# Half heads of attention between feed-forward groups, and a first token half that leads by 12 groups instead of 8

## The chip, the cores and the metric

The kernel runs on one NeuronCore of a Trainium2 chip. Its engines work from their own instruction queues, each in order: TensorE (PE; its weight loads are PEld) multiplies, VectorE (DVE), ScalarE (ACT) and GpSimd (POOL) do the rest, and SyncE (SP) issues every DMA of this kernel. The metric is the device time of one execution in microseconds (us). [...]

## The reference

Two layers over 1024 tokens of width 1024, in float32. Each layer:

```python
h = rms_norm(x) * (1 + sc1) + sh1
z = h @ w_in                        # split into the inputs of A, B and C
o_a = softmax attention             # 6 heads, 2 key heads, axial rotary, normed q and k
o_b = rms_norm(softmax(q1 k1) v - lam * softmax(q2 k2) v)   # 6 heads
o_c = gated linear recurrence, both directions              # 4 heads
x = x + g1 * (concat(o_a, o_b, o_c) @ w_out)
h = rms_norm(x) * (1 + sc2) + sh2
x = x + g2 * (square(relu(h @ w_ff1)) @ w_ff2)              # 1024 -> 4096 -> 1024
```

The six vectors sh1, sc1, g1, sh2, sc2, g2 of a layer are a modulation: `silu(c) @ w_mod + b_mod`. A last rms_norm ends the program.

## The kernel before

Activations lie with features on the 128 partitions and tokens along the free side, in two halves of 512 tokens. Weight products run as three float32r matmuls (`mm3`, L301 to L303): a high and a low part of the weights (`w_hi`, `w_lo`) against a high and a low part of the activations. A weight unit of 128x1024 (`wunit`) is one DMA of 512 KB on SP into `w_raw`, a cast on ACT (L295) and a subtraction on POOL (L297).

In a layer the token list `ORDER` names the jobs in program order: projections, early B heads, the recurrence `C`, then attention. `A01` is the pair 0 of A heads for the second token half, `B21` pair 2 of B heads for the second half, and so on. A block of 128 queries is a score product (L464), a maximum on DVE (L470), an exponential on ACT (L472), transposes on PE (L488) copied out by ACT or DVE (L489), and the product with V (L496). A B head has two score products a block and combines the two probability tiles on DVE (L604) or POOL. Scores use two buffers in PSUM.

Behind attention stand the output projection of the first half (`out_proj(0, ...)`), its norm (`norm_mod`), and the feed-forward part in 16 groups of two 128-wide blocks. A group of one half is a first product `ff1` (48 matmuls), squared relu, and a second product `ff2` (48 matmuls, added to x on DVE at L1150, or L1154 where it uses the wide PSUM tiles). With `LH = 8` the first half does groups 0 to 6 alone; then comes the second half's projection, group 7, then groups 8 to 15 for both halves with one load of their weights (`ffn_both`), and last groups 0 to 7 for the second half, their weights loaded a second time. `hook` issues the next layer's modulation, two of twelve pieces after each of six shared groups: a piece is eight DMAs of 256 KB (`mw`) and eight DVE multiply-adds (L234).

Program order is not the order that runs. A scheduler goes through a modelled timeline and gives each engine the earliest instruction in the program that is ready, so later work fills gaps of earlier work, with some parts raised (`hp`). All attention stood ahead of the first half's projection and feed-forward in the program, and they fill its gaps. The scheduler's result is fixed when the kernel is built; every engine then runs its list in order, and waits where the model was wrong.

Of the kernel before, what the change touches and what calls it, by code (L numbers as in the profile page):

```python
# [36 lines left out]
XAT, SAT = 4, 7  # L37
NIN = 4
MB = 9
LH = 8  # L40
OPRE = (3, 4, 5)
DEFER = (False, False)
MODAUX = 0
# [11 lines left out]
FORD = "xawn"  # L55
HP = {"C": 1000, "in": 1000, "post": 1000, "start": 3000, "start1": 1200}
ORDER = """b0 m lm v0 m B00 v1 bk1 m bq1 m bk2 B10 bq2 B20 lb m ff m fb m ci ak aq0 aq1
aq2 m cq0 cg0 cq1 cg1 C A00 A10 A20 A01 A11 A21 B01 B21 B11"""
RAWA = 1
BPOOL = ((1, 1, 1), (1, 1, 1))  # L60
MWB = 2
# [97 lines left out]
def tile_hybrid_encoder(ctx: ExitStack, tc: tile.TileContext, I, out, depth=DEPTH, dbg=None):  # L159
# [358 lines left out]
    def attention_a(ap, l, heads, hq):  # L518
        s = scr[l]
        hs = slice(hq * HALF, (hq + 1) * HALF)  # L520
        for h in heads:
            g = h // 3
            if ap.get("ag") != (g, hq):
                ap["ag"] = (g, hq)
                ks = ap["kst"].tile([P, S], F32R, name="ks", tag="kst")
                for i in range(2):
                    dma(ks.bitcast(F32)[64 * i:64 * i + 64, :], s.ak[i, g * 64:(g + 1) * 64, :])
                ap["ak"], ap["av"] = ks, load_v(ap, s, g)
            ks, vt = ap["ak"], ap["av"]
            if h % 2 == 0:  # L530
                ap["o"] = ap["O"].tile([P, HALF], F32, name="o", tag="o")
                ap["rr"] = ap["sm"].tile([P, 8], F32, name="rr", tag="rr", bufs=2)
            o, rr = ap["o"], ap["rr"]
            src = s.aq[h // 2]
            qs = []
            for i in range(2):
                q = ap["qst"].tile([P, HALF], F32R, name="qs", tag="qst")
                for r in range(2):
                    dma(q.bitcast(F32)[64 * r:64 * r + 64, :], src[i, (h % 2) * 64:(h % 2) * 64 + 64, hs])
                qs.append(q)  # L540
            pts = []
            for qp in range(2):
                pts.append(pt_tiles(ap))
                for qb in range(2):
                    b = 2 * qp + qb
                    c = (h % 2) * 4 + b
                    col = ap["sm"].tile([P, 4], F32, name="col", tag="col")
                    with hp('sm'):
                        p = sm_exp(ap, sm_scores(qs, ks, slice(b * P, (b + 1) * P)), col[:, 0:1], rr[:, c:c + 1])
                    with hp('ts'):  # L550
                        transpose_out(p, pts[qp], qb, (nc.scalar.copy, nc.vector.tensor_copy))
            with hp('pv'):
                pv(vt, pts, o, h % 2)
            if h % 2 == 1:
                nc.vector.reciprocal(rr, rr)
                rp = auxt()
                rt = token_rows(ap, rr, AF.Copy, 1.0, rp)
                for b in range(4):
                    nc.tensor.matmul(rp[:, b * P:(b + 1) * P], sel[:, b, :], rt, start=True, stop=True)
                nc.vector.tensor_mul(o, o, rp)  # L560
                for q in range(2):
                    o_store(ap["tp"], o, slice(q * 256, q * 256 + 256), l, h // 2, hq)

    def attention_b(ap, l, lamc, subg, heads, hq):
        s = scr[l]
        hs = slice(hq * HALF, (hq + 1) * HALF)
        for h in heads:
# [17 lines left out]
            for qp in range(2):  # L585
                pts.append(pt_tiles(ap))
                for qb in range(2):
                    b = 2 * qp + qb
                    sl = slice(b * P, (b + 1) * P)
                    c = (h % 2) * 4 + b  # L590
                    col = ap["sm"].tile([P, 4], F32, name="col", tag="col")
                    nm1, nm2, z2, r2 = [col[:, i:i + 1] for i in range(4)]
                    z1 = rr[:, c:c + 1]
                    with hp('sm'):
                        p1 = sm_exp(ap, sm_scores([st[0][0]], st[0][1], sl), nm1, z1)
                    with hp('sm'):
                        p2 = sm_exp(ap, sm_scores([st[1][0]], st[1][1], sl), nm2, z2)
                    nc.vector.reciprocal(r2, z2)
                    nc.vector.scalar_tensor_tensor(r2, z1, lamc, r2, op0=ALU.mult, op1=ALU.mult)
                    if b < BPOOL[hq][h // 2]:  # L600
                        nc.scalar.activation(p2, p2, AF.Copy, scale=r2)
                        nc.gpsimd.tensor_add(p1, p1, p2)
                    else:
                        nc.vector.scalar_tensor_tensor(p1, p2, r2, p1, op0=ALU.mult, op1=ALU.add)  # L604
                    with hp('ts'):
                        transpose_out(p1, pts[qp], qb, (nc.scalar.copy, nc.scalar.copy))
            with hp('pv'):
                pv(vt, pts, o, h % 2)
            if h % 2 == 1:
# [3 lines left out]
                for q in range(2):  # L613
# [8 lines left out]
                    rstd_tile(mp[:, 0:256], 1.0 / 64, sq, y, t, nc.gpsimd, 0.0)  # L622
                    nc.vector.scalar_tensor_tensor(o[:, cs], o[:, cs], subg, y, op0=ALU.mult, op1=ALU.mult)
                    o_store(tp, o, cs, l, 3 + h // 2, hq)


    def silu_store(tp, ps, half, dst, scale):
# [287 lines left out]
    for l in range(depth):  # L915
# [136 lines left out]

        def attend(tok):
            k, pr, hq = tok[0], int(tok[1]), int(tok[2])
            with hp("att"):
                if k == "A":
                    attention_a(ap, l, (2 * pr, 2 * pr + 1), hq)
                else:
                    ap["ag"] = None
                    attention_b(ap, l, lamc, subg, (2 * pr, 2 * pr + 1), hq)  # L1060

        def load_o(half, pool, rows, oT=None):
            if oT is None:
# [6 lines left out]
        for tok in ORDER.split():  # L1070
# [16 lines left out]
                    scan_c(c_["c"], b_["c"], l, pc[:, 3:4], lambda: early.append(early_weights()))  # L1087
                bctx.close()
            elif tok[0] in "AB":
                attend(tok)  # L1090
            else:
                jobs[tok]()

# [60 lines left out]
                        nc.vector.scalar_tensor_tensor(x, sp[:, k * HALF:k * HALF + n], g2[:, j - 1 + k:j + k], x,  # L1154
                                                       op0=ALU.mult, op1=ALU.add)

        def ffn_half(xh, h, groups, wide, finish=None):
            groups = list(groups)
            if not groups:
                return  # L1160
            prev = ff1(h, w1_units(groups[0]))
            for k, g in enumerate(groups):
                nxt = ff1(h, w1_units(groups[k + 1])) if k + 1 < len(groups) else None
                w2 = w2_units(g)
                if finish is None or nxt is not None:
                    ff2(xh, w2, prev, wide)
                else:
                    for c0 in range(0, HALF, TAILW):
                        ff2(xh, w2, prev, wide, c0, TAILW)
                        finish(slice(c0, c0 + TAILW))  # L1170
                prev = nxt

        def ffn_both(xa, ha, xb, hb, groups, hook):
# [18 lines left out]
            tiles = norm_tiles(npool)  # L1192
            if not last:
                nxt.append(norm_out(h_["h"]))
            ffn_half(xb, hb, range(LH), True, lambda cs: tail(1, xb, cs, tiles))

        nxt = []

        def tail(half, xh, cs=slice(0, HALF), tiles=None):
# [14 lines left out]
            for j in range(KT):  # L1214
# [5 lines left out]
                    nc.vector.scalar_tensor_tensor(x, x, fing[:, j:j + 1], y, op0=ALU.mult, op1=ALU.mult)  # L1220
                dma(out[j * P:(j + 1) * P, ts], x)

        def hook(g):
            modulation_sums()
            if l + 1 < depth and 0 <= g - LH < 6:
                modulation(l + 1, mpool, (2 * (g - LH), 2 * (g - LH) + 1), False)

        x0, h0 = out_proj(0, f_["x"], o_["h"], heads0, [j for j in range(KT) if j not in OPRE])
        ffn_half(x0, h0, range(LH - 1), False)
        actx.close()  # L1230
        hctx, h_ = open_pools([("h", f"h{l + 1}", 2 if last else 4, B)])
        xctx, x_ = open_pools([("x", f"xb{l}", KT, B)] + ([] if last else [("m", f"m{l}", 1, B)]))
# [65 lines left out]
```

## Time and profile before

| | |
|---|---|
| median of 3 runs | 3336.83 us (3336.62 to 3339.34) |
| the profiled execution | 3341.17 us, its span 3339.4 us |
| PE busy | 3154.9 us, 94% |
| DVE, ACT, POOL busy | 59%, 44%, 41% |
| mean granted clock of PE | 0.966 |

A row of the windows view gives, for a stretch of the span, its length, then the busy time and the instructions of PE, PEld, DVE, ACT and POOL, the granted clock of PE, and the share and rate of the DMA engines. A row of a timeline gives the start, the duration, engine, line, operation, what is written and read, and in brackets how long the engine stood idle before it and what it waited for. A row of the lines view gives count, busy time and mean duration in ns. Layer 0 runs to some 1710 us; its first-half projection begins at 804 us, its second-half one at 1099 us. Layer 1's begin at 2423 and 2723 us.

### The profile page before, as it was taken

What the parts mean: (1) busy time and instruction counts of PE and PEld (TensorE: products, weight loads), DVE (VectorE), ACT (ScalarE), POOL (GpSimd) and SP (SyncE); (2) the same over time, 40 slices, a digit from 0 to 9 for tenths busy, and PEclk for the clock granted to TensorE, in tenths of its full rate; (3) what the DMA queues carried; (4) which work ended last, traced back from release to release, by engine and by line L of the source; (5) the groups of instructions that cost most, each with busy time, mean ns of one, the idle gap of its engine ahead of it and who ended that gap; (6) DMA issues with size and microseconds to landing.
All of it is one profiled execution on the core that took longest, in us unless ns stands there. A gap on an engine that the chain in (4) does not pass through costs nothing. (4 is left out here: it accounts for less than half of the span.)

```text
span 3339.4 us, 44728 instructions
## 1 busy us (share of the span) xinstructions
PE 3154.9 (94%) x16561; PEld 2549.6 (76%) x16561; DVE 1979.6 (59%) x2648; ACT 1477.1 (44%) x2844; POOL 1355.8 (41%) x875
## 2 busy tenths in 40 slices
PE   5989889999899999999999998899999999999998
PEld 3978667777677888887878876777777788888786
DVE  7477866557764565546463776655567545333545
ACT  4245665656663322114233666565567423121323
POOL 3454511234345433225545642223344453333454
PEclk7989989999999999999999999899998999999999
DMA  6566356334424234413234533834343421111222
GB/s 240 166 184 209 102 163 189 105 114 143 133 86 170 89 117 136 139 57 108 94 108 135 179 121 107 245 103 133 108 130 103 146 103 63 51 51 51 80 94 80
DMA packets 215608, 411.78 MB, mean 123 GB/s; under 512 B 36056, under 2 KB 92504, under 8 KB 215392
## 3 DMA queue, kind: packets, MB, share of 16 engines
q1 hardware_dynamic: 215392, 408.93, 38.6%
q8 instruction: 131, 2.15, 0.3%
q14 instruction: 85, 0.70, 0.1%
HBM read 335.43 MB, written 73.40 MB: 122 GB/s over the span
## 5 line engine op out<-in xcount | busy, mean ns | idle before, releaser
L297 POOL TENSOR_TENSOR w_lo<-w_raw,w_hi 128x1024 fp32r<-128x1024 f32 x272 | 665.6, 2455 | 695.3 <-ACT w_hi L295 662.3
L301 PE MATMUL mm<-h_hi,w_hi 128*128 128x512 f32 x1472 | 596.9, 407 | 16.3 <-ACT h_hi L363 9.2
L302 PE MATMUL mm<-h_lo,w_hi 128*128 128x512 f32 x1472 | 587.0, 399 | 10.7 <-POOL h_lo L366 4.1
L303 PE MATMUL mm<-h_hi,w_lo 128*128 128x512 f32 x1472 | 582.9, 397 | 1.3 <-POOL w_lo L297 1.3
L295 ACT CAST w_hi<-w_raw 128x1024 fp32r<-128x1024 f32 x272 | 281.2, 1048 | 623.2 <-PE S L302 245.2
L470 DVE TENSOR_REDUCE col<-S 128x1 f32<-128x1024 f32 x288 | 348.1, 1220 | 158.7 <-PE S L464 157.7
L1154 DVE SCALAR_TENSOR_TENSOR x<-S,modc,x 128x512 f32<-128x512 f32 (+1 forms) x416 | 283.4, 725 | 229.5 <-PE S L303 229.3
L472 ACT ACTIVATE pr<-S,col 128x1024 f32<-128x1024 f32 x288 | 323.3, 1123 | 131.5 <-DVE col L470 64.8
L1131 DVE TENSOR_TENSOR ff_r<-ff_r 128x512 f32<-128x512 f32 x128 | 184.4, 1442 | 306.5 <-ACT act L1130 306.0
L301 PEld LDWEIGHTS mm<-h_hi,w_hi 128*128 128x128 f32 x1472 | 282.6, 192 | 87.7 <-ACT h_hi L363 11.2
L302 PEld LDWEIGHTS mm<-h_lo,w_hi 128*128 128x128 f32 x1472 | 281.9, 192 | 83.5 <-POOL h_lo L366 6.3
L303 PEld LDWEIGHTS mm<-h_hi,w_lo 128*128 128x128 f32 x1472 | 281.5, 191 | 64.9 <-POOL w_lo L297 2.0
L1132 POOL TENSOR_TENSOR act<-ff_r,act 128x512 fp32r<-128x512 f32 x128 | 168.7, 1318 | 399.0 <-DVE ff_r L1131 397.2
L301 PE MATMUL S<-act,w_hi 128*128 128x512 f32 (+1 forms) x832 | 318.8, 384 | 3.1 <-DVE x L1154 2.9
L302 PE MATMUL S<-act,w_hi 128*128 128x512 f32 (+1 forms) x832 | 317.6, 382 | 1.5 <-POOL act L1132 1.5
L303 PE MATMUL S<-act,w_lo 128*128 128x512 f32 (+1 forms) x832 | 314.9, 382 | 0.8 <-POOL w_lo L297 0.8
L464 PE MATMUL S<-ks,qs 128*128 128x512 f32 x768 | 247.6, 431 | 33.2 <-ACT pr L472 17.6
L488 PE MATMUL aux<-cst,pr 128*128 128x128 f32 x1536 | 235.0, 288 | 24.8 <-DVE pr L604 8.8
L1129 ACT ACTIVATE ff_r<-mm 128x512 f32<-128x512 f32 x128 | 76.1, 595 | 400.4 <-PE mm L303 392.7
L488 PEld LDWEIGHTS aux<-cst,pr 128*128 128x128 f32 x1536 | 189.2, 148 | 71.2 <-issue 17.5
L416 PE MATMUL mm<-w_hi,h_hi 128*128 128x256 f32 x640 | 186.3, 292 | 16.1 <-ACT z L639 10.6
L496 PE MATMUL aux<-pt,vt 128*64 128x256 f32 x1536 | 198.6, 385 | 1.5 <-ACT pt L489 1.5
(234 smaller groups left out, 5832.2 us busy)
## 6 DMA issues: line engine op xcount, KB each, us to landing
w_raw<-in_w_ff SPq DMA_DIRECT2D x192, 512.0 KB, 3.3
mw<-in_w_mod SPq DMA_DIRECT2D x160, 256.0 KB, 3.0
ks<-bk SPq DMA_DIRECT2D x192, 128.0 KB, 3.1
lf<-g_st SPq DMA_DIRECT2D x64, 256.0 KB, 2.8
oT<-o SPq DMA_DIRECT2D x64, 256.0 KB, 5.1
lf<-lf SPq DMA_DIRECT2D x16, 1024.0 KB, 5.3
w_raw<-in_w_out SPq DMA_DIRECT2D x32, 512.0 KB, 3.4
w_raw<-in_w_feat SPq DMA_DIRECT2D x28, 512.0 KB, 4.0
```

The costliest lines, as they stand in the source:

```text
L295: nc.scalar.copy(hi, raw)
L297: nc.gpsimd.tensor_sub(lo, raw, hi.bitcast(F32))
L301: nc.tensor.matmul(ps, wh, ah, start=first, stop=False)
L302: nc.tensor.matmul(ps, wh, al, start=False, stop=False)
L303: nc.tensor.matmul(ps, wl, ah, start=False, stop=last)
L416: nc.tensor.matmul(o, hi[:, kt, ts], uh[:, ws], start=kt == 0, stop=False)
L464: nc.tensor.matmul(sp[:, hh * HALF:(hh + 1) * HALF], q[:, sl], ks[:, hh * HALF:(hh + 1) * HALF], start=i == 0, stop=i == len(qs) - 1)
L470: nc.vector.tensor_reduce(nm, sp, axis=AX.X, op=ALU.max, negate=True)
L472: nc.scalar.activation(p, sp, AF.Exp, bias=nm, accum_out=z)
L488: nc.tensor.transpose(tp[:, j * P:(j + 1) * P], p[:, kt * P:(kt + 1) * P], ident)
L496: nc.tensor.matmul(ps[64 * c:64 * c + 64, 0:256], vt[:, kt, :], pts[c][kt // 4][:, kt % 4, :], start=kt == 0, stop=kt == KT - 1)
L1154: nc.vector.scalar_tensor_tensor(x, sp[:, k * HALF:k * HALF + n], g2[:, j - 1 + k:j + k], x, op0=ALU.mult, op1=ALU.add)
```

## The change

`LH` goes from 8 to 12: the first half does groups 0 to 10 alone, four groups are shared, and the second half does twelve at the end. Of the second half's attention only `A01` stays in `ORDER`; `LATE` holds the other five pairs. `attention_a` and `attention_b` become generators that stop after each half head (two query blocks), so a pair is four units and `LATE` twenty. Four units follow the first-half projection, and `between` gives out the other sixteen evenly over 23 places: after each `ff1` and after each `ff2` of the first half's groups. The modulation's pieces are dealt singly: two after each of the first two shared groups, one after each of the others, and the rest in the last twelve groups (`behind`, every second place).

```diff
-LH = 8
+LH = 12
 ORDER = """b0 m lm v0 m B00 v1 bk1 m bq1 m bk2 B10 bq2 B20 lb m ff m fb m ci ak aq0 aq1
-aq2 m cq0 cg0 cq1 cg1 C A00 A10 A20 A01 A11 A21 B01 B21 B11"""
+aq2 m cq0 cg0 cq1 cg1 C A00 A10 A20 A01"""
+LATE = "B01 A11 B21 A21 B11"
+AFTER_OUT = 4
...
+                if qp == 0:
+                    yield
             with hp('pv'):
                 pv(vt, pts, o, h % 2)
...
+            yield
...
-        def ffn_half(xh, h, groups, wide, finish=None):
+        def ffn_half(xh, h, groups, wide, finish=None, between=lambda: None):
...
             prev = ff1(h, w1_units(groups[0]))
+            between()
             for k, g in enumerate(groups):
                 nxt = ff1(h, w1_units(groups[k + 1])) if k + 1 < len(groups) else None
+                between()
                 w2 = w2_units(g)
...
+                between()
                 prev = nxt
...
-            ffn_half(xb, hb, range(LH), True, lambda cs: tail(1, xb, cs, tiles))
+            ffn_half(xb, hb, range(LH), True, lambda cs: tail(1, xb, cs, tiles), behind)
...
+        mleft = [] if last else list(range(12))
+        turn = [0]
+        def mod_next():
+            modulation_sums()
+            if mleft:
+                modulation(l + 1, mpool, (mleft.pop(0),), False)
         def hook(g):
-            modulation_sums()
-            if l + 1 < depth and 0 <= g - LH < 6:
-                modulation(l + 1, mpool, (2 * (g - LH), 2 * (g - LH) + 1), False)
+            for _ in range(2 if g - LH < 2 else 1):
+                mod_next()
+        def behind():
+            turn[0] += 1
+            if turn[0] % 2 == 0:
+                mod_next()
+        late = (u for tok in LATE.split() for u in attend(tok))
+        nlate = 4 * len(LATE.split()) - AFTER_OUT
+        slots = 2 * (LH - 1) + 1
+        done = [0, 0]
+        def between():
+            done[0] += 1
+            while done[1] * slots < done[0] * nlate and done[1] < nlate:
+                next(late)
+                done[1] += 1
         x0, h0 = out_proj(0, f_["x"], o_["h"], heads0, [j for j in range(KT) if j not in OPRE])
-        ffn_half(x0, h0, range(LH - 1), False)
+        for _ in range(AFTER_OUT):
+            next(late)
+        ffn_half(x0, h0, range(LH - 1), False, None, between)
+        for _ in late:
+            pass
```

The lines of the changed kernel stand a little lower: L488 is L490 there, L464 L466, L301 L303, L470 L472, L604 L609, L338 L340, L1111 L1119, L293 L295.

First place: PE in layer 0, from the last matmul of the first-half projection (it reads `oT`) to the first of the feed-forward part (it reads `h_hi`). `S` are scores, `cst,pr` transposes, `pt,vt` the product with V, `n_acc` the norm's sum. Before:

```order
L303 MATMUL mm<-oT,w_lo 128x512
L488 MATMUL aux<-cst,pr 128x128 x4
L464 MATMUL S<-ks,qs 128x512 x2
L488 MATMUL aux<-cst,pr 128x128 x4
L464 MATMUL S<-ks,qs 128x512 x2
L488 MATMUL aux<-cst,pr 128x128 x8
L464 MATMUL S<-ks,qs 128x512 x2
L340 MATMUL mm<-n_acc,cst 128x512
L496 MATMUL aux<-pt,vt 64x256 x16
L464 MATMUL S<-ks,qs 128x512 x4
L488 MATMUL aux<-cst,pr 128x128 x8
L464 MATMUL S<-ks,qs 128x512 x4
```

The same place of the changed kernel:

```order
L305 MATMUL mm<-oT,w_lo 128x512
L498 MATMUL aux<-pt,vt 64x256 x16
L490 MATMUL aux<-cst,pr 128x128 x4
L466 MATMUL S<-ks,qs 128x512 x4
L342 MATMUL mm<-n_acc,cst 128x512
L490 MATMUL aux<-cst,pr 128x128 x4
L466 MATMUL S<-ks,qs 128x512 x4
L490 MATMUL aux<-cst,pr 128x128 x8
L466 MATMUL S<-ks,qs 128x512 x6
L303 MATMUL mm<-h_hi,w_hi 128x512 x2
```

The filler is about as much as before, and differently placed: the product with V has moved ahead of the norm's sum.

Second place: DVE in layer 0, from the last residual add of that projection (`x`) to the norm's first step behind its sum. Before:

```order
L1111 SCALAR_TENSOR_TENSOR x<-mm,modc_73,x 128x512
L598 RECIPROCAL col<-col 128x1
L470 TENSOR_REDUCE col<-S 128x1
L599 SCALAR_TENSOR_TENSOR col<-rr,lam_0_518,col 128x1
L604 SCALAR_TENSOR_TENSOR pr<-pr,col 128x1024
L338 TENSOR_TENSOR n_acc<-n_acc,n_sq 128x512
L470 TENSOR_REDUCE col<-S 128x1 x2
L598 RECIPROCAL col<-col 128x1
L599 SCALAR_TENSOR_TENSOR col<-rr,lam_0_518,col 128x1
L311 TENSOR_SCALAR n_acc<-mm 128x512
```

In the changed kernel:

```order
L1119 SCALAR_TENSOR_TENSOR x<-mm,modc_73,x 128x512
L340 TENSOR_TENSOR n_acc<-n_acc,n_sq 128x512
L501 COPY o<-aux 64x256
L472 TENSOR_REDUCE col<-S 128x1 x2
L313 TENSOR_SCALAR n_acc<-mm 128x512
```

The attention work between the residual add and the last sum of squares is gone from there; two reduces still stand ahead of the norm's next step.

Third place: SP in layer 0, where the next layer's modulation is loaded (`mw`) beside the feed-forward weights (`w_raw`). Before, in the shared groups:

```order
L223 DMA mw<-in_w_mod 128x512 x16
L293 DMA w_raw<-in_w_ff 128x1024 x4
L223 DMA mw<-in_w_mod 128x512 x16
L293 DMA w_raw<-in_w_ff 128x1024 x4
L223 DMA mw<-in_w_mod 128x512 x16
```

In the changed kernel, in the second half's groups at the end of the layer:

```order
L225 DMA mw<-in_w_mod 128x512 x6
L295 DMA w_raw<-in_w_ff 128x1024 x2
L225 DMA mw<-in_w_mod 128x512
L295 DMA w_raw<-in_w_ff 128x1024
L225 DMA mw<-in_w_mod 128x512 x2
L295 DMA w_raw<-in_w_ff 128x1024
L225 DMA mw<-in_w_mod 128x512 x5
L295 DMA w_raw<-in_w_ff 128x1024 x2
L225 DMA mw<-in_w_mod 128x512
```

There are now four weight units to eight modulation loads, where there were four to sixteen, and the two kinds alternate.

## Rows read from the trace of the kernel before

**Rows 1.** The page's totals: busy us, share of the span, instructions of each engine.
```profile
PE 3154.9 (94%) x16561; PEld 2549.6 (76%) x16561; DVE 1979.6 (59%) x2648; ACT 1477.1 (44%) x2844; POOL 1355.8 (41%) x875
```
**Rows 2.** Windows by stage: stretch and length, then PE, PEld, DVE, ACT, POOL, PEclk, DMA.
```profile
700.00:804.40 104.40, 99.65 (x677) 77.15 (x676) 66.25 (x109) 64.04 (x167) 41.34 (x45) 0.98 0.44 130
804.40:881.20 76.80, 70.80 (x366) 54.05 (x365) 54.17 (x63) 45.42 (x79) 37.85 (x21) 1.00 0.49 148
881.20:904.90 23.70, 14.67 (x70) 8.66 (x69) 18.54 (x25) 17.32 (x29) 6.00 (x3) 0.79 0.31 92
904.90:945.00 40.10, 38.71 (x190) 29.95 (x191) 29.66 (x36) 28.66 (x49) 18.53 (x10) 0.95 0.25 79
945.00:1012.00 67.00, 67.00 (x359) 52.59 (x358) 42.66 (x58) 39.24 (x69) 30.86 (x19) 1.00 0.28 88
1012.00:1099.00 87.00, 86.47 (x377) 70.19 (x376) 37.91 (x48) 23.58 (x31) 45.46 (x25) 1.00 0.48 168
2417.00:2495.00 78.00, 76.14 (x411) 59.37 (x407) 46.86 (x59) 48.87 (x84) 37.62 (x20) 0.98 0.42 130
2495.00:2518.00 23.00, 14.88 (x57) 9.37 (x57) 20.64 (x30) 18.15 (x36) 5.84 (x6) 0.74 0.36 103
2518.00:2717.00 199.00, 196.67 (x953) 154.24 (x953) 124.07 (x146) 98.17 (x162) 99.79 (x54) 0.99 0.37 120
2800.00:3100.00 300.00, 300.00 (x1314) 246.25 (x1313) 113.32 (x137) 61.74 (x84) 103.50 (x57) 1.00 0.15 50
```
**Rows 3.** Timeline of PE in layer 0's norm stretch, at the lower clock.
```profile
885.73 1.19 PE L464 MATMUL S<-ks,qs 128*128 128x512 f32 x2 [3.94 <-DMA qs<-bq]
887.62 1.94 PE L488 MATMUL aux<-cst,pr 128*128 128x128 f32 x8 [0.69 <-DVE pr L604]
```
**Rows 4.** Timeline of PE in a feed-forward group with attention, at full clock.
```profile
962.72 1.03 PE L488 MATMUL aux<-cst,pr 128*128 128x128 f32 x8
963.51 0.48 PE L303 MATMUL mm<-h_hi,w_lo 128*128 128x512 f32 x1
963.83 0.40 PE L301 MATMUL mm<-h_hi,w_hi 128*128 128x512 f32 x1
```
**Rows 5.** Waits of PE, the longest in total: us, times, longest.
```profile
PE S L464 <- ACT pr L472: 17.6, 17, 2.0
```
**Rows 6.** Timeline of DVE in the norm stretch of layer 0, then of layer 1.
```profile
881.47 0.73 DVE L1111 SCALAR_TENSOR_TENSOR x<-mm,modc,x 128x512 f32<-128x512 f32 x1
...
887.39 0.68 DVE L338 TENSOR_TENSOR n_acc<-n_acc,n_sq 128x512 f32<-128x512 f32 x1
...
2495.76 0.74 DVE L1111 SCALAR_TENSOR_TENSOR x<-mm,modc,x 128x512 f32<-128x512 f32 x1
...
2499.02 1.08 DVE L338 TENSOR_TENSOR n_acc<-n_acc,n_sq 128x512 f32<-128x512 f32 x1
```
**Rows 7.** Timeline of POOL and DVE in layer 1's output projection.
```profile
2471.20 2.39 POOL L297 TENSOR_TENSOR w_lo<-w_raw,w_hi 128x1024 fp32r<-128x1024 f32 x1 [7.98 <-ACT w_hi L295]
2471.24 3.43 DVE L604 SCALAR_TENSOR_TENSOR pr<-pr,col 128x1024 f32<-128x1024 f32 x1
```
**Rows 8.** Timeline of PE and SP behind layer 0's last attention matmul.
```profile
1011.14 0.49 PE L621 MATMUL aux<-oq,cst 128*128 128x128 f32 x2
...
1029.08 3.48 SPq L1067 DMA_DIRECT2D oT<-o  x5
```
**Rows 9.** Lines by form, 945 to 1012 us: count, busy us, mean ns, idle before.
```profile
L470 DVE TENSOR_REDUCE col<-S 128x1 f32<-128x1024 f32 x10 | 12.1, 1218 | 2.4 <-PE S L464 2.4
L1150 DVE SCALAR_TENSOR_TENSOR x<-mm,modc,x 128x512 f32<-128x512 f32 x16 | 11.8, 744 | 5.1 <-PE mm L303 5.0
L604 DVE SCALAR_TENSOR_TENSOR pr<-pr,col 128x1024 f32<-128x1024 f32 x5 | 6.6, 1314 | 0.2
```
**Rows 10.** Timeline of SP, layer 0's shared groups.
```profile
1242.57 27.90 SPq L223 DMA_DIRECT2D mw<-in_w_mod  x16
...
1321.44 11.47 SPq L293 DMA_DIRECT2D w_raw<-in_w_ff  x4
```

More of the change, by code (lines that the diff above doesn't have):

```diff
@@ L606, in attention_b @@
                         transpose_out(p1, pts[qp], qb, (nc.scalar.copy, nc.scalar.copy))
+                if qp == 0:
+                    yield
             with hp('pv'):
@@ L624, in attention_b @@
                     o_store(tp, o, cs, l, 3 + h // 2, hq)
+            yield
     def silu_store(tp, ps, half, dst, scale):
@@ L1054, in attend @@
             k, pr, hq = tok[0], int(tok[1]), int(tok[2])
[L1055 to L1060, printed above, removed]
+            if k == "A":
+                yield from attention_a(ap, l, (2 * pr, 2 * pr + 1), hq)
+            else:
+                ap["ag"] = None
+                yield from attention_b(ap, l, lamc, subg, (2 * pr, 2 * pr + 1), hq)
         def load_o(half, pool, rows, oT=None):
@@ L1089, in tile_hybrid_encoder @@
             elif tok[0] in "AB":
-                attend(tok)
+                for _ in attend(tok):
+                    pass
             else:
@@ L1221, in tail @@
                 dma(out[j * P:(j + 1) * P, ts], x)
-        def hook(g):
-            modulation_sums()
-            if l + 1 < depth and 0 <= g - LH < 6:
-                modulation(l + 1, mpool, (2 * (g - LH), 2 * (g - LH) + 1), False)
-        x0, h0 = out_proj(0, f_["x"], o_["h"], heads0, [j for j in range(KT) if j not in OPRE])
-        ffn_half(x0, h0, range(LH - 1), False)
+        mleft = [] if last else list(range(12))
[4 more added lines that the diff above has]
+                modulation(l + 1, mpool, (mleft.pop(0),), False)
+        def hook(g):
+            for _ in range(2 if g - LH < 2 else 1):
[13 more added lines that the diff above has]
+                done[1] += 1
+        x0, h0 = out_proj(0, f_["x"], o_["h"], heads0, [j for j in range(KT) if j not in OPRE])
+        for _ in range(AFTER_OUT):
+            next(late)
+        ffn_half(x0, h0, range(LH - 1), False, None, between)
+        for _ in late:
+            pass
         actx.close()
```

## The prediction

> **What bounds the kernel now.** I read the engine totals first: TensorE is busy 3154.9 of 3339.4 us [rows 1], so at most 184 us of idle time and whatever it loses at the low clock can be had. The question is how much of that lies where the change works. The table of busy time by stage answers it [rows 2]. Its first six rows are layer 0: end of the recurrent scan, first-half output projection, the norm behind it, the first feed-forward work, the rest of the groups that still carry attention, and the pure groups up to the second output projection. Then layer 1: output projection, norm, all groups of the first half; the last row is feed-forward alone in the tail. A stage's length less its PE column is idle time.
>
> The reader is to see that attention inside feed-forward groups costs almost nothing already: 67.0 of 67.0 us busy in layer 0's third group stretch, 199.0 less 196.7 = 2.3 us idle in layer 1. The losses stand before that. Layer 0: output projection 76.8 - 70.8 = 6.0 us, norm 23.7 - 14.7 = 9.0, first groups 1.4. Layer 1: 1.9 and 23.0 - 14.9 = 8.1. The granted clock falls at the same place: 0.79 and 0.74 in the two norm stretches, 0.95 behind the first. [...] Before it fell the engine had stood still: 3.94 us ahead of a score matmul, after which eight transposes took 1.94 us [rows 3], against 1.03 us for eight at full clock [rows 4].
>
> [...]
>
> **The change part by part.**
> *Output projection.* In layer 0 PE's rows between its first and last matmul held 56 transposes, 28 score matmuls and 32 of P times V; now 28, 10 and none; in layer 1 64, 32, 32 become 12, 2, 7. Attention is what made PE wait there: the largest wait in the list, scores behind the exponential that frees their buffer, is 17 waits of about 1.0 us [rows 5]. Layer 1's 1.9 us with a full load is the nearest row for a good outcome, so layer 0 goes from 6.0 to about 1.9: -4.1 us (bounds 0 and -6.0). Layer 1: nothing.
> *Norm.* The chain from the last residual add to the first normed tile can't be moved; the filler can. In layer 0 DVE added the last column tile at 881.47 and reached the last sum of squares at 887.39, 5.9 us later, with attention's reduce and combine between; in layer 1 the same took 2495.76 to 2499.02, 3.3 us [rows 6]. In the changed order of DVE nothing stands between those two in layer 0, but the square on ACT is still needed. One add and one square are some 1.4 us, so 5.9 becomes about 2. The PE filler behind the last projection matmul (16 P times V, 16 transposes, 14 scores before the first feed-forward matmul) is about what it was. I take -4 us for layer 0 (bounds +2 and -9.0) and 0 for layer 1, whose order has as many DVE rows in the chain as before (bounds +3 and -8.1).
> [...]
> *Groups with attention.* The last score matmul stood 210 (layer 1: 234) feed-forward matmuls into the first half's 672; now it stands 582 (774) into 1056. At 300/1314 = 0.228 us a matmul [rows 2] that is 85 and 123 us more of mixed work. The idle rate of layer 1's groups, 2.3 in 199 us, makes that +2.4; I write +3 (bounds 0 and the rival below).
> *Switches.* After transposes a matmul starts 0.32 us before the next instead of 0.23 [rows 4], 0.09 each. Counted over PE's whole order there are 1087 changes of kind before and 1108 after: +1.9 us.
> *Scan.* A pair of B heads now stands in the scan where an A pair stood. B has twice the reduces for the same transposes. That stage idles 4.8 of 104.4 us and DVE is at 63% there [rows 2]; I take +1 a layer, +2 (bounds 0 and +6).
> *Weights.* Four more groups a layer are loaded twice: 32 more units of 512 KB, 32 x 2.39 us [rows 7] = 76 us of POOL. In the tail, POOL is busy 103.5 of 300 us and PE idles 0 [rows 2]; cost 0, and if the cover failed it would be the queue rival below.
> *Wait added.* Second-half projection now follows layer 1's last attention by 156 matmuls, 35 us (before 348, 79 us). In layer 0 the last attention matmul began at 1011.14, and the last of the sixteen loads of its output left the queue by 1032.56 [rows 8]: 21 us. The cover holds; with one such chain more behind it, some 10 us would be lost once.
>
> Sum: -4.1 - 4 - 6 + 3 + 1.9 + 2 = -7.2 us. The profiled run took 3341.17 us (span 3339.4), 4.3 over the median of 3336.83. 3341.17 - 7.2 = 3334.0, less 4.3 is 3329.7; I say 3329.
>
> [...] DVE's combine of two probability tiles takes 1.31 us on average [rows 9], but one that began 0.04 us after a weight subtraction on POOL took 3.43 [rows 7]: 2.39 of POOL's time and its own 1.0. [...]
>
> **Rivals.**
> 1. *The loss only stays put.* [...] For it: both layers lose 8 to 9 us in the norm though their fillers differ. Then -4 and -6 go: -7.2 + 10 = +2.8, 3340 against the median; without the scan and group terms 3335. I put this case at 3335 to 3340, no change.
> 2. *DVE becomes the bound in the second feed-forward product: slower.* Before, attention had precedence over all feed-forward work and filled both products; now the first product of a group is ahead of the half head behind it, and in layer 1's order 48 matmuls in a row carry no attention, so a group's attention falls into the other 48 (10.9 us). There DVE has 8 residual adds x 0.744 = 6.0 and, for some 0.7 of a B head, 5.6 reduces x 1.218 + 2.6 combines x 1.314 = 10.2 [rows 9], 16.2 us before POOL's holds; PE has 10.9 + 8.5 (a head's attention matmuls are about 12 us). It decides when DVE with its holds passes 19.4 us, which takes 1.4 holds of 2.4. If each of some 16 such products then waits 1.5 us (one or two waits of the size of [rows 5]) it costs 24 us in place of the 3: -7.2 + 21 = +13.8, 3351. Against it: 67 us without idle at DVE 64% in layer 0 [rows 2], and an order that sets 6 to 12 feed-forward matmuls between most score pairs.
> 3. *The load queue starves layer 0's last groups.* Six modulation pieces now run beside the doubled weight loads. On SP sixteen of their loads took 27.9 us and four weight loads 11.5 [rows 10]: 14.0 + 11.5 = 25.5 us a group against 96 x 0.228 = 21.9. Six groups fall behind by 21 us. Four units in store, one group's work, cover most, and the changed order mixes the two kinds, so their waits overlap. I price it at +8: the gain is gone, 3337.
> [...]
> That the change isn't done as described holds in part: the scheduler pulls the first two late pieces (B01 and A11) ahead of the projection, so three are spread, over about six to eight of the eleven groups.
>
> **Numbers.** Forecast (3321 to 3332) 0.42, rival 1 0.20, rival 2 0.17, rival 3 0.08, rival 4 0.13. What can be told from no change is 0.2%, 6.7 us: faster means below 3330.2, slower above 3343.5. Rival 4 and most of the forecast (0.38) make 0.51 faster; rivals 1 and 3 and the rest of the forecast 0.32 same; rival 2 0.17 slower. The likeliest case alone is 3321 to 3332. The range has to hold most of rivals 1, 3 and 4 and the near part of 2: 3312 to 3348.
>
> **What would show it.** Right: in the changed profile layer 0's output projection idles about 2 us, its norm stretch about 5, and the clock there is nearer 0.9; the groups with attention idle under 2 us a layer. Wrong: a norm stretch of 9 us idle at 0.79 (rival 1); DVE near 90% with score waits behind the exponential all along the groups (rival 2); weight waits of TensorE in the last groups of layer 0 (rival 3); or idle time ahead of layer 1's second output projection (the cover).

## The result, and the profile after

The changed kernel took 3358.22 us (median of six runs, 3352.48 to 3374.21); the kernel before, on the same chip in turn with it, 3338.45 (3336.62 to 3350.75). The ratio is 1.0069, 95% interval 1.0048 to 1.0090: slower by some 20 us. The forecast was 3329, with 3312 to 3348 as its range.

The run that was profiled with the comparison is the slowest of the six (3374.21), so the same kernel was profiled once more: 3359.24 us, near the median. "After" below is this second profile, 18.1 us above the profiled run of before (3341.17). Its line numbers lie 2 to 8 above those of before. Its totals, against [rows 1]:
```profile
PE 3161.0 (94%) x16561; PEld 2549.5 (76%) x16561; DVE 2021.8 (60%) x2648; ACT 1509.1 (45%) x2876; POOL 1447.3 (43%) x907
```
The same 16561 matmuls and 2648 VectorE instructions; GpSimd has 32 more, the doubled weight units. Its windows by stage (columns as in [rows 2]): layer 0's scan, output projection, norm, two stretches of groups; then layer 1's scan, projection, norm and groups.
```profile
535.91:807.75 271.84, 263.85 (x1746) 204.90 (x1745) 170.88 (x276) 176.47 (x506) 95.64 (x110) 0.99 0.42 123
807.75:866.40 58.65, 51.60 (x232) 41.67 (x230) 31.73 (x36) 27.70 (x46) 32.55 (x18) 0.94 0.55 166
866.40:890.10 23.70, 20.13 (x95) 14.62 (x95) 22.54 (x31) 18.56 (x32) 4.97 (x4) 0.78 0.42 122
890.10:930.20 40.10, 40.10 (x200) 30.95 (x199) 22.75 (x25) 19.56 (x35) 18.29 (x13) 1.00 0.24 79
930.20:1030.00 99.80, 99.80 (x503) 78.35 (x502) 56.76 (x67) 44.53 (x71) 45.78 (x25) 1.00 0.32 101
...
2163.24:2434.99 271.75, 262.55 (x1725) 204.26 (x1724) 167.26 (x276) 176.61 (x505) 93.55 (x109) 0.98 0.44 130
2434.99:2482.60 47.61, 47.61 (x223) 38.73 (x222) 15.15 (x17) 17.39 (x26) 27.89 (x15) 1.00 0.38 126
2482.60:2505.60 23.00, 16.06 (x91) 10.29 (x90) 21.09 (x27) 17.00 (x30) 8.12 (x5) 0.90 0.32 106
2505.60:2704.60 199.00, 199.00 (x987) 155.52 (x987) 123.36 (x140) 97.05 (x159) 89.32 (x49) 0.99 0.31 98
```
And the two scans of the kernel before, from the first main matmul of the scan to the first one of the output projection:
```profile
536.37:804.45 268.08, 263.29 (x1765) 205.38 (x1765) 161.23 (x261) 167.03 (x487) 90.66 (x108) 0.99 0.40 121
2151.25:2423.00 271.75, 268.71 (x1807) 209.33 (x1805) 158.25 (x263) 169.33 (x488) 87.44 (x106) 0.99 0.39 121
```
Read the layer 1 scan first: 271.75 us in both kernels, but 1725 TensorE instructions where there were 1807. The stage is as long and does 82 instructions less, and VectorE is busy 9 us longer in it. What the scan no longer does, the groups behind it must. Length alone hides this, so the table takes from each stage's length what its matmuls cost at full clock (count of a kind by its spacing in the timelines where the granted clock is 1.00: 0.2265 us for 512 columns, 0.0985 a transpose, 0.1125 P times V, 0.1 the scan's small ones), and then the same of before. A price is a typical spacing, so a cell is an estimate good to 1 or 2 us and a sum to 3 or 4. The runs behind the columns come from several chips, while the profile of before is one run (3341.17); "elsewhere" is for the most part the start of the program.

| us lost, against before | after | late_a_first | b01_early | b01_single | lead12_only | lead12_again |
|---|---|---|---|---|---|---|
| scan, layer 0 / 1 | +7.4 / +9.9 | +1.5 / -1.7 | +9.5 / +14.9 | 0 / +5.2 | +0.7 / -4.6 | +3.0 / -5.3 |
| projection, norm, groups, layer 0 | +1.3 | +3.0 | -2.5 | -3.6 | +4.0 | +4.1 |
| the same, layer 1 | -5.4 | -2.8 | -8.9 | -8.0 | -0.8 | -0.6 |
| layer 0's tail | +3.5 | +2.6 | -0.6 | -0.6 | +2.5 | +3.6 |
| layer 1's input projection | +0.5 | +0.2 | -0.8 | +0.6 | +3.1 | +8.1 |
| elsewhere | -0.4 | -6.8 | -4.9 | -0.4 | -5.7 | -4.9 |
| time of that run | 3359.24 | 3340.40 | 3351.55 | 3327.05 | 3340.62 | 3350.51 |

In the first column the two scans lose 17.3 us, and the whole column is 16.8: what the other stages lose and gain cancels, with 5.4 gained in layer 1 behind its scan. Layer 0's tail has one wait that before has only in small. The timeline of TensorE after, then of before, at the first group that only the second half runs:
```profile
1469.35 0.39 PE L303 MATMUL S<-act,w_hi 128*128 128x512 f32 x1
1476.06 0.80 PE L304 MATMUL S<-act,w_hi 128*128 128x512 f32 x1 [6.32 <-POOL act L1140]
1476.65 0.63 PE L305 MATMUL S<-act,w_lo 128*128 128x512 f32 x1
```
```profile
1560.45 0.51 PE L302 MATMUL S<-act,w_hi 128*128 128x512 f32 x1 [1.54 <-POOL act L1132]
```
6.3 us against 1.5, and behind it the matmuls stand 0.43 us apart in place of 0.23. The first profile (3374.21 us) has the same wait, 6.35 us up to 1476.98, and the same spacing behind it; its granted clock is 0.50 from 1476.50 to 1481.50 and 1.00 from 1482.50 to 1490.00. Half-microsecond windows of that profile and of before read 0.50 or 1.00, save where the clock changes; the low clock below is 0.50, the full clock 1.00. What held the activation up, on VectorE and GpSimd after:
```profile
1463.08 5.38 DVE L370 SCALAR_TENSOR_TENSOR h_lo<-x,modc,h_hi 128x512 fp32r<-128x512 f32 x8
1468.38 1.28 DVE L1139 TENSOR_TENSOR ff_r<-ff_r 128x512 f32<-128x512 f32 x2
1469.65 2.49 DVE L234 TENSOR_SCALAR macc<-mw,cond 128x512 f32<-128x512 f32 x1
1472.18 2.71 DVE L236 SCALAR_TENSOR_TENSOR macc<-mw,cond,macc 128x512 f32<-128x512 f32 x1
1477.53 2.59 DVE L1139 TENSOR_TENSOR ff_r<-ff_r 128x512 f32<-128x512 f32 x1 [2.64 <-ACT act L1138]
```
```profile
1464.57 9.77 POOL L299 TENSOR_TENSOR w_lo<-w_raw,w_hi 128x1024 fp32r<-128x1024 f32 x2 [7.25 <-ACT w_hi L297]
1474.30 2.95 POOL L1140 TENSOR_TENSOR act<-ff_r,act 128x512 fp32r<-128x512 f32 x2
```
The norm that closes the first half (`h_lo`), GpSimd's subtraction of two weight units and a modulation piece (`macc`, the eighth of twelve) fall together. Two subtractions take 9.77 us, where 304 of them average 2.49, and the activation, whose input VectorE has ready at 1469.7 (`ff_r`), is queued behind them. In before the modulation is done by then, and GpSimd stands idle ahead of the activation, which waits for VectorE alone:
```profile
1558.69 1.71 POOL L1132 TENSOR_TENSOR act<-ff_r,act 128x512 fp32r<-128x512 f32 x1 [4.54 <-DVE ff_r L1131]
```

### The profile page after: what moved, and what is told of

It reads as the page before. It is cut to its first block, busy times and chain, and to the rows that moved or that the text cites. A ratio compares the mean times of both kernels' runs of the same rounds, so it can differ in the third digit from the quotient of the medians.

```text
span 3372.4 us, 44919 instructions
## 1 busy us (share of the span) xinstructions
PE 3173.3 (94%) x16561; PEld 2554.2 (76%) x16561; DVE 2020.6 (60%) x2648; ACT 1507.4 (45%) x2876; POOL 1448.4 (43%) x907
## 5 line engine op out<-in xcount | busy, mean ns | idle before, releaser
L299 POOL TENSOR_TENSOR w_lo<-w_raw,w_hi 128x1024 fp32r<-128x1024 f32 x304 | 756.7, 2498 | 777.2 <-ACT w_hi L297 724.9
L297 ACT CAST w_hi<-w_raw 128x1024 fp32r<-128x1024 f32 x304 | 314.2, 1048 | 789.9 <-PE S L304 288.4
L303 PE MATMUL mm<-h_hi,w_hi 128*128 128x512 f32 x1472 | 595.5, 406 | 14.6 <-ACT h_hi L365 8.4
L304 PE MATMUL mm<-h_lo,w_hi 128*128 128x512 f32 x1472 | 586.1, 398 | 11.4 <-POOL h_lo L368 4.8
L472 DVE TENSOR_REDUCE col<-S 128x1 f32<-128x1024 f32 x288 | 347.7, 1219 | 142.5 <-PE S L466 140.9
L1139 DVE TENSOR_TENSOR ff_r<-ff_r 128x512 f32<-128x512 f32 x128 | 207.2, 1619 | 276.9 <-ACT act L1138 272.8
L1162 DVE SCALAR_TENSOR_TENSOR x<-S,modc,x 128x512 f32<-128x512 f32 (+1 forms) x352 | 238.0, 720 | 183.9 <-PE S L305 183.8
L303 PEld LDWEIGHTS mm<-h_hi,w_hi 128*128 128x128 f32 x1472 | 282.0, 192 | 86.0 <-ACT h_hi L365 9.5
L466 PE MATMUL S<-ks,qs 128*128 128x512 f32 x768 | 249.2, 435 | 32.5 <-ACT pr L474 13.8
L304 PE MATMUL S<-act,w_hi 128*128 128x512 f32 (+1 forms) x704 | 269.0, 382 | 6.3 <-POOL act L1140 6.3
L303 PE MATMUL S<-act,w_hi 128*128 128x512 f32 (+1 forms) x704 | 269.3, 384 | 1.2 <-DVE x L1162 0.9
L305 PE MATMUL S<-act,w_lo 128*128 128x512 f32 (+1 forms) x704 | 265.9, 382 | 0.5 <-POOL w_lo L299 0.5
L490 PE MATMUL aux<-cst,pr 128*128 128x128 f32 x1536 | 232.3, 287 | 29.9 <-ACT pt L491 10.3
L490 PEld LDWEIGHTS aux<-cst,pr 128*128 128x128 f32 x1536 | 187.5, 147 | 75.6 <-ACT pt L491 15.7
L1158 DVE SCALAR_TENSOR_TENSOR x<-mm,modc,x 128x512 f32<-128x512 f32 x176 | 130.7, 748 | 139.1 <-PE mm L305 138.3
L498 PE MATMUL aux<-pt,vt 128*64 128x256 f32 x1536 | 209.8, 393 | 1.5 <-ACT pt L491 1.5
```

Of the source, the lines that this page charges most:

```text
L297: nc.scalar.copy(hi, raw)
L299: nc.gpsimd.tensor_sub(lo, raw, hi.bitcast(F32))
L303: nc.tensor.matmul(ps, wh, ah, start=first, stop=False)
L304: nc.tensor.matmul(ps, wh, al, start=False, stop=False)
L305: nc.tensor.matmul(ps, wl, ah, start=False, stop=last)
L466: nc.tensor.matmul(sp[:, hh * HALF:(hh + 1) * HALF], q[:, sl], ks[:, hh * HALF:(hh + 1) * HALF], start=i == 0, stop=i == len(qs) - 1)
```

## The experiments

Ratios are to the kernel before on the same chip, with 95% intervals. Theories: *scan* (a pair of B heads in the scan is the loss), *lead* (12 groups led, so doubled loads and half of the modulation beside single groups), *spread* (half heads in the groups). Orders of pieces are abridged to their ends.

**late_a_first**: the changed kernel, only with an A pair as the first late piece.
```
-LATE = "B01 A11 B21 A21 B11"
+LATE = "A11 A21 B01 B21 B11"
```


> The changed kernel with one string permuted: LATE is A11 A21 B01 B21 B11, so the scheduler again fills the recurrent scan with A pairs only (its PE rows ahead of the first output projection hold the same 308 scores, 600 transposes and 288 products with V in layer 0 as the kernel before). Theory scan (a B pair as filler slows the scan and starves PE there): the scan goes back to 268 and 272 us from 274 and 280, the time to 3335 to 3343, 15 to 20 us under the changed kernel. Theory lead (doubled weight loads and alternating queue in the tail): still 3353 to 3360. Theory spread (giving attention out in half heads makes the groups slow): still 3353 to 3360.

3346.68 us, 1.0028 [1.0018, 1.0039], between the two times expected. The scans are back (269.0 and 266.4 us), and with them more than half of the loss.

**b01_early**: the kernel before, only with B01 ahead of A11 and A21.
```
-A20 A01 A11 A21 B01 B21 B11
+A20 A01 B01 A11 A21 B21 B11
```


> The kernel before with one pair moved in its list: B01 ahead of A11 and A21, nothing else, so the scan's filler is that of the changed kernel while lead and feed-forward stay as before. Theory scan: 8 to 16 us slower than before, 3346 to 3354, with PE idle in the scan up from 4 to 8 or more. Theories lead and spread: no change, 3335 to 3341.

3351.25 us, 1.0039 [1.0024, 1.0054]. One pair moved, nothing spread, nothing loaded twice: 13 us. Its scans, and layer 1's longest wait of TensorE in it:
```profile
531.96:808.10 276.14, 265.12 (x1753) 205.21 (x1753) 170.95 (x271) 173.15 (x502) 93.59 (x109) 0.99 0.41 121
2152.63:2433.89 281.26, 271.43 (x1747) 211.31 (x1746) 168.00 (x280) 177.54 (x509) 92.45 (x109) 0.96 0.43 126
```
```profile
PE aux L488 <- DVE pr L604: 3.2, 3, 2.0
```
VectorE has 10 us more of work in each. In layer 1 TensorE's longest wait is for the combine of two probability tiles, and the clock of the scan is 0.96 against 0.99: some 17 us more at the low clock, an estimate from the two clocks and lengths, half of which is lost (spacing 0.43 us for 0.23): 8 of the 14.9 us there. In layer 0 the longest wait is another, one of 3.1 us for a load (`vp<-cv`). The stages behind the scans gain 11.4 of the 24.4 us back, so the move costs 13 us in all.

**lead12_only** and **lead12_again**: the changed kernel with the order of before, twice.
```
-LATE = "B01 A11 B21 A21 B11"   AFTER_OUT = 4
+LATE = ""                      AFTER_OUT = 0
```


> The changed kernel with LATE empty and the old ORDER: lead of 12 groups, doubled weight loads and the dealt modulation, but attention all ahead of the projection as before. Theory scan: within 5 us of before, 3336 to 3343. Theory lead: most of the loss stays, 3350 to 3358, with a stall of some 6 us in the second product behind layer 0's shared groups. Theory spread: as before, 3336 to 3343.

> The lead of 12 groups alone once more, for a profile nearer its median of 3351 than the first (3340.6, its fastest). [...]

3351.25 us, 1.0036 [1.0023, 1.0049]; again 3350.51. The lead costs 12 us by itself, and the wait for the activation is there too (6.1 us). The first profile was of its fastest run (3340.62); against it the second loses 2.3 us more in layer 0's scan, with, by my count, 14 us at the low clock there against 3, and 5.0 in layer 1's input projection, where the time at the low clock is about the same. So neither the low clock nor waits alone explain it.

**spread_lead8**: the changed kernel with LH = 8.

> The changed kernel with LH = 8: half heads spread over seven groups, B01 in the scan as in the changed kernel, weights loaded as before. Theory scan: the loss stays, 3350 to 3360. Theory lead: gone, 3335 to 3342. Theory spread: stays or grows, since the same half heads fall into fewer groups, 3355 to 3365.

3389.09 us, 1.0146 [1.0129, 1.0163], above every time expected. Seven groups don't hold the half heads: the second output projection begins at 1111.52 and 2757.51 (before 1099.03 and 2722.56), and TensorE waits for the last attention's output in it, in layer 0 and in layer 1:
```profile
PE mm L303 <- DMA oT<-o: 17.2, 1, 17.2
```
```profile
PE mm L303 <- DMA oT<-o: 10.2, 1, 10.2
```
Spread in this way, the half heads need a longer lead.

**a_first_lead10**: late_a_first with LH = 10.

> The changed kernel with A11 as the first late piece, so that an A pair stands in the scan as before, and a lead of 10 groups in place of 12 (with 12: 3347 measured). If the cost of the lead is in proportion to its groups: 3338 to 3342. If the lead costs only beyond what the queue can hold: 3334 to 3338, a little faster than before by the three microseconds that the even spreading gave. If the half heads no longer fit into nine groups and run over their end, as with a lead of 8: 3350 to 3390.

3352.03 us, 1.0048 [1.0031, 1.0064]: not between the leads of 8 and 12. Its profile loses some 5 us in each layer. In layer 0's tail it is the wait for the activation again. In layer 1 the half heads run over their end, as the last of the three expectations has it: the second output projection waits for attention's output, its clock falls, and it takes 50.40 us where the kernel before takes 44.80. The first line is of layer 0, the others of layer 1:
```profile
PE S L304 <- POOL act L1140: 5.9, 1, 5.9
```
```profile
PE mm L303 <- DMA oT<-o: 2.7, 2, 1.4
```
```profile
2772.60:2823.00 50.40, 48.41 (x192) 38.00 (x193) 18.90 (x13) 11.42 (x14) 20.74 (x9) 0.93 0.46 161
```
So the cost of a lead isn't proportional to its groups.

**lead12_nomod** and its control **before_nomod**: layer 1's modulation left out.
```
 lead12_nomod   -mleft = [] if last else list(range(12))
 lead12_nomod   +mleft = []
 before_nomod   -if l + 1 < depth and 0 <= g - LH < 6:
 before_nomod   +if False:
```


> The lead of 12 groups with the order of attention of the kernel before (3351 measured for that alone), and layer 1's modulation left out, loads, sums and all; it adds at most 3.6 us of TensorE work in layer 0's tail, so the kernel before without it would take some 3335 to 3338. If the twelve modulation pieces between the weight loads are what the lead costs: 3334 to 3341. If the doubled weight units are (loads, subtractions on GpSimd and SBUF traffic in both layers): 3346 to 3352.

> The kernel before with layer 1's modulation left out, loads, sums and all: the control for the lead of 12 without it (3318 measured). TensorE's own work for it is 48 matmuls of 0.25 us, 12 us. If the lead costs only because the modulation then stands beside the single groups: 3315 to 3321, as long as the lead of 12 without it, so that the modulation costs 18 us here and 33 there. If the doubled weight units cost something by themselves: 3304 to 3312. If the longer lead would even gain without it: 3322 to 3327, the time of before less the 12 us.

3318.43 us, 0.9945 [0.9933, 0.9957], and 3311.85, 0.9927 [0.9914, 0.9940]. Without modulation the lead costs 0.0018, 6 us; with it 12. The two intervals overlap, so 6 can be told neither from nothing nor from 12. The first of the two came out below both of its expectations, because leaving the modulation out is worth more than its matmuls in either kernel: 23 us in before, of which 12 are TensorE's. Not all of that need be a price of the modulation. From layer 0's first output projection to its second the kernel without it is 9.7 us shorter with as many matmuls, although of the twelve pieces of before only one stands there (its first load goes out at 822.91 us) and the sums of the others begin at 1196 us. The first row is of before, the second of before_nomod:
```profile
804.45:1099.03 294.58, 277.63 (x1356) 215.43 (x1354) 182.89 (x226) 154.20 (x257) 138.70 (x76) 0.98 0.39 127
```
```profile
807.60:1092.50 284.90, 276.40 (x1355) 215.81 (x1354) 177.18 (x218) 153.60 (x258) 140.34 (x76) 0.98 0.37 121
```
The scheduler gave this stretch another order of instructions, so a run without the modulation differs by more than the modulation.

**b01_single** and its control **before_single**: B01 early, or in its old place, with the second softmax of that pair left out.
```
+one = hq == 1 and h < 2
-p2 = sm_exp(ap, sm_scores([st[1][0]], st[1][1], sl), nm2, z2)
+if not one: p2 = sm_exp(ap, sm_scores([st[1][0]], st[1][1], sl), nm2, z2)
...
+if one: pass   # no combine
```


> The kernel before with B01 moved into the scan (3351 measured), and of that piece, in the second token half, the second softmax left out: its scores, maximum, exponential and the combine on VectorE. Less TensorE work by 32 matmuls a layer, some 3.6 us each. If the scan is longer because a B head loads VectorE and ScalarE twice as much per transpose: both scans 267 to 271 us, total 3331 to 3339. If it is the loads of a B head, or the place of the piece in the order: 3343 to 3349, scans 274 or more.

> The control for b01_single (3321): B01 in its old place, behind the A pairs, with the same second softmax left out. If the second softmax's load on VectorE and ScalarE is the whole price of B01 in the scan (13 us): this takes 3318 to 3324, the same as b01_single. If a B pair in the scan costs for another reason (its loads, its place in the order): 3306 to 3313, 8 to 13 us less than b01_single.

3321.09 us, 0.9955 [0.9942, 0.9967], and 3329.53, 0.9970 [0.9959, 0.9982]; the first is below both of its expected times, the second above both. In its old place the softmax is worth 10 us, not much over TensorE's share (32 score matmuls, 7). With B01 in the scan it is worth 28 (1.0039 to 0.9955). So B01 in the scan costs 13 us with its second softmax, and without it nothing that can be told (5 us less, with overlapping intervals). The scans of b01_single (before_single's are 270.8 and 269.8 us):
```profile
535.82:800.09 264.27, 262.25 (x1754) 206.22 (x1753) 149.55 (x244) 164.52 (x490) 88.03 (x109) 0.98 0.42 128
2143.46:2417.58 274.12, 267.28 (x1786) 209.00 (x1784) 156.04 (x255) 170.56 (x498) 88.05 (x107) 0.98 0.44 131
```
VectorE is 21 us (layer 0) and 12 us (layer 1) less busy than in b01_early, ScalarE 9 and 7. The second softmax is the price: the pair's place and nearly all of its loads from memory are as in b01_early, and the cost is gone. Which part of it, its work on VectorE, on ScalarE or its score products, no run separates.

**lead12_gap**, **a_first_gap**, **lead12_sparse**, **a_first_sparse**: the modulation kept away from the pile-up, on lead12_only and on late_a_first.
```
 hook    -for _ in range(2 if g - LH < 2 else 1):
 gap     +for _ in range(2 if g - LH < 3 else 0):
 behind  -if turn[0] % 2 == 0:
 gap     +if turn[0] % 2 == 0 and turn[0] > 6:
 sparse  +if turn[0] % 4 == 0:
```


> The lead of 12 groups with the order of attention of the kernel before (3351 measured), all of the modulation done, but none of it between the last shared group and the third single group, where the first half's closing norm occupies VectorE and TensorE stood 6 us for an activation of GpSimd. If the pile-up at that place is the lead's cost in layer 0's tail: the wait is under 2 us, the stretch from the end of the second output projection to layer 0's last feed-forward matmul is 5 to 8 us shorter (478 to 481 against 485.9), and the time 3342 to 3346. If modulation beside single groups costs wherever it stands (its loads on the queue, its sums on VectorE): 3349 to 3353.

> The changed kernel with both causes taken out: A11 as the first late piece, so that an A pair stands in the scan (3347 with this alone), and no modulation between the last shared group and the third single group. If the two add up: 3336 to 3341, as before. If the spreading of the half heads gains as little as three microseconds and the lead costs by more than the pile-up: 3342 to 3346. If the place of the modulation makes no difference: 3346 to 3348.

> The lead of 12 groups alone (3351), with one modulation piece in two single groups in place of one in each, the first of them one group later. If the pile-up at the closing norm and the density are the lead's cost in layer 0's tail: no wait of TensorE over 3 us there, the stretch from the end of the second output projection 478 to 481 us against 485.9, and 3343 to 3347. If the density makes no difference: 3349 to 3353. If the later pieces only meet the weight loads elsewhere, as with the gap of three groups: above 3355.

> The changed kernel with A11 as the first late piece (3347) and one modulation piece in two single groups. If the two causes add up: 3338 to 3342, level with before. If half of the lead's cost stays whatever the modulation does, as the kernels without it have it (3318 against 3312): 3341 to 3346. If the sparse pieces cost as the gap did: above 3350.

3372.71 us (1.0111 [1.0094, 1.0128]), 3370.10 (1.0103 [1.0086, 1.0121]), 3372.98 (1.0100 [1.0082, 1.0117]) and 3369.72 (1.0084 [1.0066, 1.0102]): all four 19 to 25 us *slower* than where they started, by the ratios, so my remedy was wrong. The 6 us wait for the activation is gone in each, and layer 0's tail is 14 to 22 us longer. ScalarE's waits for weights to land, from 1180 to 1740 us, in lead12_only, lead12_sparse and lead12_gap:
```profile
ACT w_hi L297 <- DMA w_raw<-in_w_ff: 54.1, 21, 8.7
```
```profile
ACT w_hi L297 <- DMA w_raw<-in_w_ff: 116.9, 19, 10.9
```
```profile
ACT w_hi L297 <- DMA w_raw<-in_w_ff: 119.0, 18, 14.0
```
They double, and TensorE then waits for weights or for the residual adds. Its longest in the gap kernel, same stretch:
```profile
PE S L303 <- DVE x L1162: 11.9, 7, 2.7
PE mm L305 <- POOL w_lo L299: 8.3, 5, 3.5
```
A residual add (L1162) stands behind modulation sums (L236) that wait for their load and are then held up beside two weight subtractions of GpSimd (5.18 us); two sums take 5.74 us, where one alone takes 0.73. VectorE in the gap kernel:
```profile
1602.56 5.74 DVE L236 SCALAR_TENSOR_TENSOR macc<-mw,cond,macc 128x512 f32<-128x512 f32 x2 [1.23 <-DMA mw<-in_w_mod]
1608.23 1.40 DVE L1162 SCALAR_TENSOR_TENSOR x<-S,modc,x 128x512 f32<-128x512 f32 x2
```
That the load queue has no slack left in that tail is my reading of these waits; no run gives the loads another queue. Why the changed kernel's own arrangement is the one that barely fits is not shown.

## Why the prediction was wrong

**The step that failed: "Scan ... I take +1 a layer, +2 (bounds 0 and +6)".** The two scans lose 17 us in the profile after; done alone the move costs 13 us of time (b01_early). I judged a stage by idle share and VectorE's mean (63%). The scan has its own chain through VectorE, and the second softmax adds work to it: the reduces and combines stand between one score and the next transpose, and ahead of the scan's own VectorE steps. That they hold the chain up is argued from the waits of layer 1; shown is that the second softmax is the price. VectorE's work grows by 10 us in layer 0 and 9 in layer 1 (161.23 to 170.88, 158.25 to 167.26). Reduces and combines are 8.4 of it in layer 0, here before and after:
```profile
L470 DVE TENSOR_REDUCE col<-S 128x1 f32<-128x1024 f32 x53 | 64.8, 1223 | 32.2 <-PE S L464 32.0
L604 DVE SCALAR_TENSOR_TENSOR pr<-pr,col 128x1024 f32<-128x1024 f32 x3 | 6.6, 2200 | 0.0
```
```profile
L472 DVE TENSOR_REDUCE col<-S 128x1 f32<-128x1024 f32 x57 | 69.7, 1222 | 25.1 <-PE S L466 24.5
L609 DVE SCALAR_TENSOR_TENSOR pr<-pr,col 128x1024 f32<-128x1024 f32 x7 | 10.1, 1437 | 0.1
```
The smaller steps of a B head add some 9 more, and eight copies fewer, which an A head makes on VectorE and a B head doesn't, take 5.5 off. TensorE lost about as much. I had the prices of a reduce and a combine [rows 9] and didn't set them against the scan; the bound of +6 should have been some 10 a layer.

**"Weights ... cost 0" failed too.** The lead alone costs 12 us, and perhaps 6 with no modulation beside it. I gave 8 us to the rival of the load queue, with the right place (layer 0's last groups) and a chance of 0.08. What appears in the changed kernel is not yet a starved queue but the pile-up of GpSimd, VectorE and norm, 6.3 us and the low clock behind it. When that was moved, the tail lost 14 to 22 us more, with the waits for loads doubled. For the other half of the lead alone I can only say where its profiles lose: 4 us in layer 0's groups, 3 to 8 in layer 1's input projection, with 5 gained in layer 1's scan. In that input projection its order is another one (402 VectorE instructions against 392), while the changed kernel has there the order of before and loses 0.5 us. So those 3 to 8 us belong to the list that the scheduler built for this experiment, and not to the change.

**The gains came only in part.**
- *Output projection*, -4.1 forecast: 7.05 us idle in 58.65, before 6.0 in 76.8 [rows 2]. Nothing gained, and its clock fell from 1.00 to 0.94. One wait alone is 4.5 us, scores behind the exponential; 17.6 us of it in [rows 5] was spread over 17 waits. Layer 1's projection, where I wrote 0, lost its idle time altogether (47.61 of 47.61).
- *Norm*, -4: 3.6 us idle against 9.0, so -5.4. This step was right, and by its own reason: the last residual add is followed by the last sum of squares in 1.5 us (it was 5.9 in [rows 6]):
```profile
867.11 0.74 DVE L1119 SCALAR_TENSOR_TENSOR x<-mm,modc,x 128x512 f32<-128x512 f32 x1
868.60 1.78 DVE L340 TENSOR_TENSOR n_acc<-n_acc,n_sq 128x512 f32<-128x512 f32 x1 [0.76 <-ACT n_sq L336]
```
- *Clock*, -6: no run shows this term, which was my estimate. What the runs show is a granted clock of 0.78 in that stretch against 0.79 before, so nothing was had in layer 0. In the first profile of the same kernel it is 0.93 there, but 0.91 in the projection ahead of it, so the low clock moved. In layer 1, where I wrote 0 for the norm, the clock is 0.90 against 0.74, and 6.9 us are idle against 8.1.
- *Groups*, +3: 199.00 of 199.00 us busy in layer 1, 139.9 of 139.9 in layer 0's first two stretches. In the third, which before has not, 3.9 us are idle, behind ScalarE's relu and VectorE's residual adds. Little or no cost; VectorE as the bound of the second product (the rival on the slower side, 3351) did not happen, although its time came near. The half heads do hide in the groups.
```profile
1030.00:1195.00 165.00, 161.10 (x743) 126.18 (x742) 85.79 (x96) 60.55 (x90) 81.19 (x42) 1.00 0.35 121
```
- *Switches*, +1.9: no run separates it.
- *Wait added*, 0: right for a lead of 12. From 2704.60 to the second output projection TensorE idles 1.7 us.

The sum by the runs: B01 in the scan +0.0039, lead +0.0036, spreading -0.0008 (late_a_first less lead12_only, whose intervals overlap, so no gain is proved) make 1.0067, against 1.0069. So close a match is partly luck, since a part of the lead's 12 us lies where the changed kernel loses nothing. The direction was lost by two terms that I had priced near nothing; the first is shown, the second only in part.

## What to carry to other kernels

When pieces of work trade places, price each by the engine that its new neighbours chain through, not by the mean share of that engine; and compare stages by work done, since a stage can keep its length and hand its work on. A pass that "costs nothing while the cover holds" (weights loaded again beside other loads) needs the cover's slack as a number. A pile-up that is moved may land on a queue that is already full, so try the move before trusting it. And where a scheduler builds the lists, compare the order in the stages that an experiment was not meant to touch.

## What the runs showed of the hardware that was not expected

GpSimd's subtraction of one weight unit, 2.49 us on average, took 7.30 us when it began inside a chain of VectorE instructions: eight of the norm (`h_lo`) and two squarings, back to back from 1463.08 to 1469.66. It began at 1464.57 and ended 2.20 us after the chain, which is less than its usual time, while none of the ten took more than 0.74 us. I read this as a standstill until the chain was through. The other way round, a modulation sum on VectorE that began 0.36 us behind the next subtraction took 2.71 us in place of 0.74. The first profile shows the same two at the same place: 7.29 and 2.71 us. So in one pile-up an instruction of each engine took longer beside the other engine's.

The time of the same kernel follows the mean granted clock: its six runs go from 3352.48 us at 0.969 to 3374.21 at 0.963, and the four between them lie in the same order but for 0.1 us. An estimate from these two clocks: 0.006 less is 2 x 0.006 x 3360 = 40 us more at the low clock, which costs half of that, 20 of the 22 us. So a profile's stages carry a few us of clock that are not the change's.
